# One of four token tiles leaves the dense products of a routed expert layer: its experts' rows are gathered and summed on VectorE

## The chip, the cores and the metric

One core of a Trainium2 chip runs the whole program as one launch. The metric is device time in microseconds (us), the median of several executions. Engines carry the names of the profile: PE (matrix products), PEld (loading of PE's stationary operand), DVE (VectorE), ACT (ScalarE), POOL (GpSimd) and SP, whose queue issues most DMAs.

## The reference, cut to what matters

The program is a block of two layers (mixer, then a routed expert layer called PEER) over 256 tokens `x` and 256 context tokens, followed by a second block of two layers over `x` alone. The change is in the PEER of layer 0. For each token, eight heads each pick 16 of 16,384 experts, and the output is a weighted sum of the rows of the picked experts:

```
def chunk(xc):
    q = (xc @ w_q).reshape(PEER_CHUNK, PEER_HEADS, 2, PEER_HALF)
    s = jnp.einsum('thid,hikd->thik', q, sub_keys).astype(jnp.float32)
    s1, i1 = lax.top_k(s[:, :, 0], PEER_TOPK)
    s2, i2 = lax.top_k(s[:, :, 1], PEER_TOPK)
    ...
    top_s, pos = lax.top_k(cand, PEER_TOPK)
    eidx = jnp.take_along_axis(cidx, pos, axis=-1)
    gate = jax.nn.softmax(top_s, axis=-1)
    u = u_emb[eidx]
    hid = jax.nn.gelu(jnp.einsum('td,thkd->thk', xc, u))
    wgt = (gate * hid.astype(jnp.float32)).astype(xc.dtype)
    return jnp.einsum('thk,thkd->td', wgt, v_emb[eidx])
```

So a token needs 128 rows of `u_emb` and 128 rows of `v_emb`, each of 1024 float32 (4 KB).

## The kernel before, in words

**Products in float32.** Every weight tile is 128x1024 float32 (512 KB). SP's queue brings it (`raw`), ACT copies it to a rounded high part `wh` (L209), and DVE, or for some tiles POOL, subtracts to get the low part `wl` (L220). `W.pool_every` says which tiles' `wl` goes to POOL. A product is then three matmuls (`mm3`, L443 to L445: high by high, low by high, high by low).

**PEER of layer 0** works on four token tiles of 128 columns: tiles 0 and 1 are `x`, tiles 2 and 3 the context; T = 512. It doesn't gather. It computes all 16,384 experts for all tokens, and the picked ones are singled out by a matrix that is zero elsewhere:

- *Queries* (`wq`, 16 weight tiles). Beside them `topk_keys` takes the top 16 of each of 16 key groups and each token tile on DVE (L1282 to L1287).
- *The u stage*, 128 weight tiles of 24 matmuls over 512 columns each. ACT applies gelu (L1460), and the result goes to DRAM (`gel_d`). Beside it runs `route()`: candidate sums `cand` on POOL (L1309), top 16 on DVE (L1316 to L1320), index look-up by one-hot compare, multiply and reduce on DVE (`eq`, L1334 to L1337). Then the gate matrix is built, four tokens a flush: DVE makes `Am`, `Bk`, `Bm` (L1395 to L1402), PE does eight 128x128 float16 matmuls (L1379), ACT evicts to `gst` (L1380), and a DMA takes it to DRAM (`g_d`); 128 flushes in all. Still in this stage, 56 tiles of the modulation weights (`modt`: 8 of layer 0, 48 of layer 1) are each multiplied by two vectors and summed, two DVE instructions each (`mod_tile`, L491, `sjunk`).
- *The vv stage*, 128 weight tiles of 24 matmuls of 512 columns (L1497; 6 for each of four token tiles). The hidden values and gates come back from DRAM four tiles at a time (`gelc` L1421, `gmc` L1423), POOL multiplies them (`wmul`, L1430), ACT and DVE split the product (`Wh` L448, `Wl` L449).

After that, `mixer(1)` begins with 24 conv and 16 gate projections of 256 columns (`tproj`, 24 matmuls each), with elementwise work on DVE beside them (L718 to L727). Between its conv projections the context rows are normalised (`norm_ctx`, called after its first and second conv step).

**What sets the order.** Weight tiles stand in one planned list (`plan`). Side work is written as generators that a small planner (`Side`) advances after each group of matmuls (`tick`): before, by a fixed period, so many steps spread over the u stage. Each engine's queue is in the order in which the program emits instructions.

Of the kernel before, what the change touches and what calls it, by code (L numbers as in the profile page):

```python
# [10 lines left out]
F32 = mybir.dt.float32  # L11
# [8 lines left out]
D = 1024  # L20
# [17 lines left out]
AY = 10  # L38
# [18 lines left out]
LATE = [i for i in range(16, 118) if i % 2 or i % 20 == 0]  # L57


def mod_late(i):  # L60
    n = LATE.index(i)
    return (0, 40 + n) if n < 8 else (1, n - 8)
# [11 lines left out]
def plan():  # L74
# [9 lines left out]
    for l in range(NL):  # L84
# [29 lines left out]
        for i in range(128):  # L114
            order.append(("u", l, i))
            if l == 0 and i in LATE:
                order.append(("modt",) + mod_late(i))
        for i in range(128):
            order.append(("vv", l, i))
    for l in range(NL):  # L120
# [139 lines left out]
RATE = {"a": (50.0, 0.92), "v": (80.0, 1.04), "p": (100.0, 2.2)}  # L260


class Side:
# [8 lines left out]
    def __init__(self, period, ring):  # L272
        self.lanes, self.lates = [], []
        self.period, self.ring = period, ring
        self.now = self.due = 0.0
        self.slot = [0.0] * 4
        self.free = {"a": 0.0, "v": 0.0, "p": 0.0}
        self.seq = 0
        self.floor = False

# [19 lines left out]
    def use(self, eng, n):  # L300

        if eng == "e":
            return self.now + SEM
        a, b = RATE[eng]
        self.free[eng] = max(self.free[eng], self.now) + a + b * n
        return self.free[eng] + SEM

# [42 lines left out]
    def tick(self, dt):  # L350
        self.now += dt
# [29 lines left out]
def tile_dit_peer_conformer(ctx: ExitStack, tc: tile.TileContext, A, out):  # L381
# [77 lines left out]
    modc = [consts.tile([128, 48, 2], F32, name=f"modc{l}") for l in range(NL)]  # L459

# [25 lines left out]
    def mod_tile(l, n, S, junk):  # L486

        raw = W.next("modt", l, n)
        for s in range(2):
            o = modc[l][:, n, s:s + 1]  # L490
            nc.vector.scalar_tensor_tensor(junk, raw, 1.0, S[:, s], op0=OP.mult, op1=OP.mult, accum_out=o)  # L491
        made.add((l, n))
# [125 lines left out]

    def tick(dt):
# [35 lines left out]
    def mixer(l, kp, norm_ctx=None, convs=None):  # L655
# [5 lines left out]
        with ExitStack() as st:  # L661
# [46 lines left out]
            for ct in range(8):  # L708
                def proj(b):
                    p = convs[b] if convs and ct == 0 else tproj(("conv", l, ct * 3 + b), X, T)  # L710
                    md(mod_slots(ct, b))
                    return p
# [16 lines left out]
                if l == 1 and ct < 2:  # L729
                    norm_ctx[ct]()  # L730
# [14 lines left out]
            for k, n in enumerate(GATES):  # L745
                g = sig(m1, ("gate", l, 16 + n))
                md(gate_slots(k, 0))
                pco = tproj(("co", l, n), CG, T)
                md(gate_slots(k, 1))
                nc.vector.scalar_tensor_tensor(merged[:, n], g, 1.0, pco[:, :T], op0=OP.add, op1=OP.mult)  # L750
            phase.close()
            m2 = phase.enter_context(tc.tile_pool(name=f"mixb{l}", bufs=1))
# [384 lines left out]
            phase.close()  # L1137
            keys = kp.enter_context(tc.tile_pool(name=f"keys{l}", bufs=1, side="right")).tile([128, 16, 128], F32, name="keys")
# [63 lines left out]
    def seg_tail(pool, ns, upd, halves, hs, ss, ab, banks, fill=None, then=None):  # L1202
# [9 lines left out]
        if fill is None:  # L1212
# [3 lines left out]
            rest(*range(2, 2 * ns))  # L1216
# [14 lines left out]
    def peer(l, hcp, kp, keys, early):  # L1231
        last = l == NL - 1
        T = 256 if last else 512
        nt = T // 128
        ns = T // 256
        TB = 32
        ntb = T // TB
        CI = 2048 // T
        gel_d = [dram.tile([128, CI, T], F32, name=f"gel{l}_{c}") for c in range(128 // CI)]
# [3 lines left out]
        with ExitStack() as st:  # L1243
            pp = st.enter_context(tc.tile_pool(name=f"peer{l}", bufs=1))
            IT = pp.tile([128, 2, T], F16, name="IT")
            GT = pp.tile([128, 2, T], F16, name="GT")
            GN = pp.tile([128, nt, 128], F32, name="GN")
            IN = pp.tile([128, nt, 2, 128], F32, name="IN")
# [5 lines left out]
            if l == 0:  # L1254
                ms_stack = ExitStack()
                ms = ms_stack.enter_context(tc.tile_pool(name="modrow", bufs=1))
# [5 lines left out]
            tk = tk_stack.enter_context(tc.tile_pool(name=f"topk{l}", bufs=1))  # L1262
            sv = tk.tile([128, nt, 16, 16], F32, name="sv")
# [3 lines left out]

            def topk_keys():
                for c in range(16):
                    while c not in qs or (c < 2 and c + 1 not in qs):  # L1270
                        yield
                    q = qs.pop(c)
# [4 lines left out]
                    nc.scalar.activation(s, b[:, :T], AF.Copy)  # L1277
                    for t in range(nt):
                        yield
# [8 lines left out]
                    yield  # L1288
# [6 lines left out]
            side = cur["side"] = W.side = Side(24 * T / 2.4 / (nt + 1.3), ring)  # L1295
            side.add(select())
            W.pool_every = 1
            for c in range(16):
                p = early.pop(0)[0] if early else tproj(("wq", l, c), X, T)
                q = tk.tile([128, T], F32, name="q", bufs=4)  # L1300
                nc.scalar.activation(q, p[:, :T], AF.Copy)
                qs[c] = q

            def route():
                for t in range(nt):
                    v4 = sv[:, t].rearrange("p (h i) k -> p h i k", i=2)
                    cand = tk.tile([128, 8, 16, 16], F32, name="cand", bufs=1)
                    for h in range(8):
                        nc.gpsimd.tensor_add(cand[:, h], v4[:, h, 0, :, None].to_broadcast([128, 16, 16]),  # L1309
                                             v4[:, h, 1, None, :].to_broadcast([128, 16, 16]))  # L1310
                    ts = tk.tile([128, 8, 16], F32, name="ts", bufs=2)
                    pos = tk.tile([128, 8, 16], U32, name="pos", bufs=2)
                    yield
                    for h in range(8):
# [6 lines left out]
                        yield TKW  # L1321
                    ab = tk.tile([128, 2, 8, 16], U32, name="ab", bufs=2)
                    nc.vector.tensor_scalar(ab[:, 0], pos, 4, None, op0=OP.logical_shift_right)
                    nc.vector.tensor_scalar(ab[:, 1], pos, 15, None, op0=OP.bitwise_and)
                    abf = tk.tile([128, 2, 8, 16], F32, name="abf", bufs=2)
                    nc.vector.tensor_copy(abf, ab)
                    sif = tk.tile([128, 8, 2, 16], F32, name="sif", bufs=2)
                    nc.vector.tensor_copy(sif, si[:, t].rearrange("p (h i) k -> p h i k", i=2))
                    yield
                    for i in range(2):  # L1330
                        for h0 in (0, 4):
# [6 lines left out]
                            yield TKW * 1.3  # L1338
                    nc.vector.tensor_sub(GN[:, t].rearrange("p (h k) -> p h k", h=8), ts, ts[:, :, 0:1].to_broadcast([128, 8, 16]))
                nc.scalar.activation(GN, GN, AF.Exp)  # L1340
                sm = tk.tile([128, nt, 8], F32, name="smx")
                for t in range(nt):
                    g = GN[:, t].rearrange("p (h k) -> p h k", h=8)
                    nc.vector.tensor_reduce(sm[:, t], g, axis=AX.X, op=OP.add)
                nc.vector.reciprocal(sm, sm)
                for t in range(nt):
                    g = GN[:, t].rearrange("p (h k) -> p h k", h=8)
                    nc.vector.tensor_mul(g, g, sm[:, t, :, None].to_broadcast([128, 8, 16]))
                yield
                yield  # L1350
                yield
                for i in range(3):
                    b = bankB()
                    for t in range(nt):
                        src = GN[:, t] if i == 2 else IN[:, t, i]
                        nc.tensor.transpose(b[:, t * 128:(t + 1) * 128], src, ident)
                    if i < 2:
                        nc.scalar.activation(IT[:, i], b[:, :T], AF.Copy)
                        continue
                    gw = tk.tile([128, T], F32, name="s", bufs=2)  # L1360
                    nc.scalar.activation(gw, b[:, :T], AF.Copy, scale=GSCALE)
                    nc.scalar.activation(GT[:, 0], gw, AF.Copy)
                    nc.vector.tensor_sub(GT[:, 1], gw, GT[:, 0])
                W.pool_every = 0
# [6 lines left out]
                def flush(q, Am, Bm):  # L1371
# [8 lines left out]
                    nc.scalar.activation(sg[:, :, r * 4:r * 4 + 4].rearrange("p i t -> p t i"),  # L1380
                                         b.rearrange("p (t i) -> p t i", t=4), AF.Copy, scale=1.0 / GSCALE)
                    if r == TB // 4 - 1:
                        nc.scalar.dma_start(g_d[tb], sg)

# [831 lines left out]
```

## Time and profile before

| | |
|---|---|
| median of three runs | 4619.03 us (4615.78, 4619.03, 4619.39) |
| profiled execution | 4620.17 us, of which the span of the trace is 4618.4 us |
| PE busy | 4520.1 us (98%) |
| DVE busy | 3002.5 us (65%) |
| ACT busy | 2022.4 us (44%) |
| POOL busy | 959.8 us (21%) |
| DMA | 831.69 MB, 180 GB/s mean |

The profile gives each engine's busy time, the span in 40 slices, the DMA queues, the chain that ended last and groups of instructions by line. The trace behind it also answers for any stretch: busy time by stretch, who waited for whom, and single instructions in order of time. Times in stretches count from the span's start.

### The profile page before, as it was taken

Reading aid. Unit: us, or ns where it says so; the run is one execution under the profiler, and the core shown is the slowest. Engines: PE = TensorE matmul, PEld = TensorE weight load, DVE = VectorE, ACT = ScalarE, POOL = GpSimd, SP = SyncE. Lnnn points to the kernel's source line nnn. Section 1 sums busy time; section 2 is a strip of 40 time slices with the busy share of each in tenths; the row PEclk is TensorE's granted clock in tenths of the full one; section 3 lists DMA queues with packets and bytes.
Section 4 is the critical chain, followed back from the end, with each engine's and each line's share of the span. In section 5 each row is a group of like instructions: output and inputs, shape, how many; then the busy total and the mean of one; then the engine's idle time right before and its main releaser. Section 6 shows DMA issues by size and latency. Waiting matters only on the chain. (4 is left out here: it accounts for less than half of the span.)

```text
span 4618.4 us, 67755 instructions
## 1 busy us (share of the span) xinstructions
PE 4520.1 (98%) x26426; PEld 3890.3 (84%) x26426; DVE 3002.5 (65%) x4853; ACT 2022.4 (44%) x2955; POOL 959.8 (21%) x772
## 2 busy tenths in 40 slices
PE   8999999999999999999999989999999999999999
PEld 5887878887777888888898879999887998999988
DVE  6747768899987333333365878786666577555855
ACT  4224443224665322222244444576444445444544
POOL 0012433331001322222222446201443000000000
PEclk9999999999999999999999989999999999999999
DMA  5532232455667655555543336678886644556344
GB/s 213 167 99 67 71 107 87 142 187 203 252 248 254 203 193 192 186 184 187 165 152 122 101 121 205 225 272 304 286 282 234 211 152 128 187 178 210 116 157 154
DMA packets 284922, 831.69 MB, mean 180 GB/s; under 512 B 23720, under 2 KB 108088, under 8 KB 275128
## 3 DMA queue, kind: packets, MB, share of 16 engines
q1 hardware_dynamic: 260384, 713.64, 47.0%
q10 hardware_dynamic: 24040, 112.66, 6.5%
q8 instruction: 207, 3.39, 0.3%
q14 instruction: 115, 0.94, 0.1%
q0 software_dynamic: 176, 1.06, 0.1%
HBM read 724.50 MB, written 102.77 MB: 179 GB/s over the span
## 5 line engine op out<-in xcount | busy, mean ns | idle before, releaser
L220 DVE TENSOR_TENSOR wl<-raw,wh 128x1024 fp32r<-128x1024 f32 (+1 forms) x959 | 1206.3, 1267 | 844.3 <-PE pB L1497 340.7
L209 ACT ACTIVATE wh<-raw 128x1024 fp32r<-128x1024 f32 (+1 forms) x1086 | 1131.8, 1045 | 1075.8 <-issue 697.8
L443 PE MATMUL pA<-xH,wh 128*128 128x256 f32 (+1 forms) x4600 | 1504.0, 327 | 2.9 <-ACT xH L448 1.3
L445 PE MATMUL pA<-xH,wl 128*128 128x256 f32 (+1 forms) x4600 | 1480.2, 322 | 4.7 <-DVE wl L220 3.0
L444 PE MATMUL pA<-xL,wh 128*128 128x256 f32 (+1 forms) x4600 | 1479.0, 322 | 0.5 <-DVE xL L449 0.3
L445 PEld LDWEIGHTS pA<-xH,wl 128*128 128x128 f32 x4600 | 872.7, 190 | 77.8 <-DVE wl L220 4.6
L443 PEld LDWEIGHTS pA<-xH,wh 128*128 128x128 f32 x4600 | 870.4, 189 | 75.7 <-issue 6.0
L444 PEld LDWEIGHTS pA<-xL,wh 128*128 128x128 f32 x4600 | 870.4, 189 | 68.8 <-DVE xL L449 1.1
L1430 POOL TENSOR_TENSOR gelc<-gelc,gmc 128x512 f32<-128x512 f32 (+1 forms) x256 | 333.8, 1336 | 982.1 <-DMA gmc<-gmat 663.6
L220 POOL TENSOR_TENSOR wl<-raw,wh 128x1024 fp32r<-128x1024 f32 (+1 forms) x127 | 316.0, 2488 | 874.9 <-PE pA L445 499.0
L1497 PE MATMUL pA<-wh,Wh 128*128 128x512 f32 x1024 | 322.5, 395 | 0.0
L1497 PE MATMUL pA<-wl,Wh 128*128 128x512 f32 x1024 | 322.5, 395 | 0.0
L1497 PE MATMUL pA<-wh,Wl 128*128 128x512 f32 x1024 | 322.5, 395 | 0.0
L444 PE MATMUL pA<-wl,xH 128*128 128x256 f32 (+2 forms) x800 | 271.6, 339 | 8.6 <-POOL wl L220 6.0
L443 PE MATMUL pA<-wh,xH 128*128 128x256 f32 (+2 forms) x800 | 277.4, 347 | 1.1 <-ACT xH L448 1.0
L1380 ACT ACTIVATE gst<-pB 128x512 f32<-128x512 f32 x192 | 215.1, 1126 | 140.3 <-PE pB L1379 139.6
L449 DVE TENSOR_TENSOR Wl<-gelc,Wh 128x512 fp32r<-128x512 f32 (+1 forms) x256 | 162.4, 635 | 169.7 <-ACT Wh L448 167.7
L445 PE MATMUL pA<-wh,xL 128*128 128x256 f32 (+2 forms) x800 | 270.9, 339 | 1.1 <-DVE xL L449 1.1
L1460 ACT ACTIVATE gstage<-pA 128x512 f32<-128x512 f32 x192 | 117.1, 610 | 289.0 <-PE pA L445 276.4
L1497 PEld LDWEIGHTS pA<-wh,Wl 128*128 128x128 f32 x1024 | 192.0, 187 | 47.0
L1497 PEld LDWEIGHTS pA<-wl,Wh 128*128 128x128 f32 x1024 | 192.0, 188 | 46.8
L1497 PEld LDWEIGHTS pA<-wh,Wh 128*128 128x128 f32 x1024 | 192.0, 188 | 46.7
(425 smaller groups left out, 6004.2 us busy)
## 6 DMA issues: line engine op xcount, KB each, us to landing
raw<-in_u SPq DMA_DIRECT2D x256, 512.0 KB, 4.2
raw<-in_vv SPq DMA_DIRECT2D x256, 512.0 KB, 3.7
gel<-gstage ACTq DMA_DIRECT2D x96, 512.0 KB, 4.0
gmat<-gst ACTq DMA_DIRECT2D x24, 2048.0 KB, 8.2
gelc<-gel SPq DMA_DIRECT2D x48, 1024.0 KB, 5.9
gmc<-gmat SPq DMA_DIRECT2D x48, 1024.0 KB, 9.6
raw<-in_modt SPq DMA_DIRECT2D x80, 512.0 KB, 4.0
raw<-in_conv SPq DMA_DIRECT2D x48, 512.0 KB, 3.6
```

What stands on the lines that cost most here:

```text
L209: self.nc.scalar.activation(h[:, :w], t[:, :w], AF.Copy)
L220: e.tensor_sub(lo[:, :w], t[:, :w], h[:, :w].bitcast(F32))
L443: nc.tensor.matmul(o, s[0], m[0], start=start, stop=False)
L444: nc.tensor.matmul(o, s[0], m[1], start=False, stop=False)
L445: nc.tensor.matmul(o, s[1], m[0], start=False, stop=stop)
L449: nc.vector.tensor_sub(lo, src, h.bitcast(F32))
L1380: nc.scalar.activation(sg[:, :, r * 4:r * 4 + 4].rearrange("p i t -> p t i"), b.rearrange("p (t i) -> p t i", t=4), AF.Copy, scale=1.0 / G ...
L1430: nc.gpsimd.tensor_mul(gv, gv, m[:, :, ci])
L1460: nc.scalar.activation(gs[:, j:j + n].rearrange("p a t -> p (a t)"), b, AF.Gelu_apprx_tanh)
L1497: nc.tensor.matmul(acc[t][dh], s_, m_[:, dh * 512:(dh + 1) * 512], start=(i == 0 and n == 0), stop=(i == 127 and n == 2))
```

## The change: what it does

Token tile 3, the second context tile, leaves the dense products of layer 0's PEER. TD = 384 columns stay in the u stage, three token tiles (18 matmuls for a weight tile) in the vv stage, 96 flushes in the gate matrix; `gel_d` and `g_d` shrink by a quarter. `route()` handles tile 3 first and turns its picks into expert numbers `gi`. A generator `gathered()` then takes, for each of the 128 picks, one row of `u` for each of the 128 tokens by an indirect DMA issued on POOL (512 KB, into one of four buffers `gr`), and a DVE instruction forms the dot products with the tokens' rows `gx`; then gelu and gate; then the same with rows of `v`, which a DVE instruction adds, times the weight, to the accumulator. That is 256 indirect DMAs and 256 DVE instructions over 128x1024. `gx`, the tile's rows, comes from 16 small matmuls.

With it: the planner knows DVE's and ACT's rates and fills DVE up to its estimated end (`spend`, `RATE2`, `pe = 1.09`); `cand` goes from POOL to DVE; `wmul` goes from POOL to one DVE instruction of 128x1536 for four tiles; layer 1's 48 modulation tiles go from the u stage to the vv stage, 32 of them with one column in place of two; the tables of `angles` (POOL) go from the u stage's end to its last tiles and the vv stage; the `wl` of the vv stage stays on DVE. What is left of the gathers at the end of the vv stage is spread over the first 34 projections of `mixer(1)` (`tail`, `TAIL = 35`); tile 3's update comes at projection 34, the context's row factors at 35, its columns at 38.

```diff
-LATE = [i for i in range(16, 118) if i % 2 or i % 20 == 0]
...
+LATE = [60 + 7 * i for i in range(8)]
+def late_v(i):
+    n = (i - 1) * 48 // 122
+    return (n,) if 0 < i <= 122 and n < i * 48 // 122 else ()
...
+RATE2 = {"a": (120.0, 0.92), "v": (165.0, 1.04), "p": (100.0, 2.2)}
+NG = 4
+GLAT = 4500.0
+TAIL = 35
...
-        for s in range(2):
+        for s in range(2 if l == 0 or n < 16 else 1):
...
+                if tail:
+                    tail(ct * 3 + b, m1)
...
-                if l == 1 and ct < 2:
-                    norm_ctx[ct]()
...
+        TD = T - 128 if sp else T
+        ntd = TD // 128
...
+            def gathered():
+                tabs = (A["ur"], A["vr"])
...
+                        nc.gpsimd.indirect_dma_start(t, None, tabs[j // 128], bass.IndirectOffsetOnAxis(ap=gi[:, k:k + 1], axis=0))
+                        rows[j] = (t, side.free["v"] + GLAT)
...
+                for j in range(128):
+                    yield step(1.0, rows[j][1])
+                    r = rows.pop(j)[0]
+                    nc.vector.scalar_tensor_tensor(r, r, 1.0, gx, op0=OP.mult, op1=OP.mult, accum_out=gz[:, j:j + 1])
...
+                    fetch(j + NG)
+                nc.scalar.activation(gz, gz, AF.Gelu_apprx_tanh)
...
+                for j in range(128):
+                    yield step(1.0, rows[128 + j][1])
...
+                        nc.vector.scalar_tensor_tensor(acc, r, gz[:, j:j + 1], acc, op0=OP.mult, op1=OP.add)
...
+                    fetch(128 + j + NG)
...
-                for t in range(nt):
+                for t in (range(nt) if not sp else (3, 0, 1, 2)):
...
+                    nc.vector.tensor_mul(gv, gv, m.rearrange("p b c t -> p c b t"))
...
-                    mm3(o, (h[:, d * 128:(d + 1) * 128], lo[:, d * 128:(d + 1) * 128]), (X[0][:, d, :T], X[1][:, d, :T]), d == 0, d == 7)
-                    tick(3 * T / 2.4)
...
+                    mm3(o, (h[:, d * 128:(d + 1) * 128], lo[:, d * 128:(d + 1) * 128]), (X[0][:, d, :TD], X[1][:, d, :TD]), d == 0, d == 7)
+                    tick(3 * TD / 2.4)
...
-                for t in range(nt):
+                for t in range(ntd):
                     vmm(t, i, w, hl)
...
+            while ga["n"] < 256 and (256 - ga["n"]) * TAIL > (TAIL - 1 - n) * todo:
+                next(gat_gen, None)
```

On DVE, in the middle of layer 0's vv stage, two instructions a weight tile stood before (`wl` is the low part of the weight tile, `Wl` that of the hidden values):

```order
L449 TENSOR_TENSOR Wl<-gelc,Wh 128x512
L220 TENSOR_TENSOR wl<-raw,wh 128x1024
```

and at the same place there are now gathers (`gr`), modulation (`sjunk`) and the gate product (`gmc`) between them:

```order
L1604 TENSOR_TENSOR gelc<-gelc,gmc 128x1536
L473 TENSOR_TENSOR Wl<-gelc,Wh 128x384
L223 TENSOR_TENSOR wl<-raw,wh 128x1024
L1408 SCALAR_TENSOR_TENSOR gr,gz<-gr,gx 128x1024
L516 SCALAR_TENSOR_TENSOR sjunk,modc_98<-raw,S 128x1024 x2
L473 TENSOR_TENSOR Wl<-gelc,Wh 128x384
L223 TENSOR_TENSOR wl<-raw,wh 128x1024
L473 TENSOR_TENSOR Wl<-gelc,Wh 128x384
L223 TENSOR_TENSOR wl<-raw,wh 128x1024
L1408 SCALAR_TENSOR_TENSOR gr,gz<-gr,gx 128x1024 x2
```

A `wl` that PE will load now stands behind up to four instructions over 128x1024 where it stood behind one over 128x512.

On DVE, in the conv projections at the head of `mixer(1)`, before:

```order
L220 TENSOR_TENSOR wl<-raw,wh 128x1024
L718 TENSOR_TENSOR upad_18242<-pA,tmpa 128x256
L722 TENSOR_SCALAR tmpb<-upad_18242,pcol 128x256
L724 SCALAR_TENSOR_TENSOR tmpb<-upad_18242,pcol,tmpb 128x256 x2
L727 SCALAR_TENSOR_TENSOR tmpb<-tmpb,pA 128x256
L449 TENSOR_TENSOR cgL<-tmpb,cgH 128x256
L220 TENSOR_TENSOR wl<-raw,wh 128x1024 x2
```

and now, with the last gathers of the second half (`gx` is the accumulator):

```order
L223 TENSOR_TENSOR wl<-raw,wh 128x1024
L1423 SCALAR_TENSOR_TENSOR gx<-gr,gz,gx 128x1024 x2
L223 TENSOR_TENSOR wl<-raw,wh 128x1024
L1423 SCALAR_TENSOR_TENSOR gx<-gr,gz,gx 128x1024
L750 TENSOR_TENSOR upad_17554<-pA,tmpa 128x256
L223 TENSOR_TENSOR wl<-raw,wh 128x1024
L1423 SCALAR_TENSOR_TENSOR gx<-gr,gz,gx 128x1024 x2
L754 TENSOR_SCALAR tmpb<-upad_17554,pcol 128x256
L756 SCALAR_TENSOR_TENSOR tmpb<-upad_17554,pcol,tmpb 128x256 x2
L759 SCALAR_TENSOR_TENSOR tmpb<-tmpb,pA 128x256
L473 TENSOR_TENSOR cgL<-tmpb,cgH 128x256
```

One or two gather instructions have come between each pair of `wl`.

## Rows read from the trace of the kernel before

**Rows 1.** The page's head: span; busy us of each engine, share, instructions.
```profile
span 4618.4 us, 67755 instructions
PE 4520.1 (98%) x26426; PEld 3890.3 (84%) x26426; DVE 3002.5 (65%) x4853; ACT 2022.4 (44%) x2955; POOL 959.8 (21%) x772
```

**Rows 2.** Busy time by stretch: queries, u stage, vv stage, first projections of mixer(1).
```profile
core 0: us, PE busy (x) PEld busy (x) DVE busy (x) ACT busy (x) POOL busy (x), PEclk, DMA share, GB/s
717.00:816.00 99.00, 99.00 (x503) 82.89 (x502) 85.49 (x437) 33.15 (x47) 36.03 (x15) 1.00 0.27 86
816.00:1600.90 784.90, 784.90 (x4114) 621.23 (x4113) 631.05 (x1001) 353.52 (x402) 152.08 (x157) 1.00 0.62 213
1600.90:2320.30 719.40, 718.92 (x3089) 577.49 (x3087) 285.18 (x270) 206.60 (x267) 178.28 (x122) 1.00 0.55 183
2326.00:2449.00 123.00, 118.17 (x953) 116.72 (x953) 78.83 (x112) 57.30 (x83) 21.35 (x19) 0.97 0.56 175
```

**Rows 3.** Waits, 700 to 2480 us, PE; then 1605 to 2300 us, DVE.
```profile
engine line waited for: us in total, times, longest us
PE pA L444 <- DVE xL L449: 2.4, 5, 0.7
PE pA L445 <- DVE wl L220: 1.9, 2, 1.1
...
DVE wl L220 <- PE pB L1497: 333.5, 123, 2.8
```

**Rows 4.** Timeline, PE: first and 48th of consecutive 384-column matmuls, second block.
```profile
start us, us, engine line op out<-in xcount [idle before <-releaser]
3799.71 0.34 PE L443 MATMUL pA<-wh,xH 128*128 128x384 f32 x1
...
3807.85 0.34 PE L445 MATMUL pA<-wh,xL 128*128 128x384 f32 x1
```

**Rows 5.** Busy time in a stretch, PE, the gate-matrix matmuls (L1379) alone.
```profile
1108.00:1480.00 372.00, 81.03 (x1024) 1.00 0.69 249
```

**Rows 6.** Groups by line and shape, u and vv stage (816 to 2320 us).
```profile
line engine op names shapes xcount | busy us, mean ns | idle before us <-releasers
L220 DVE TENSOR_TENSOR wl<-raw,wh 128x1024 fp32r<-128x1024 f32 x229 | 309.8, 1353 | 470.2 <-PE pB L1497 340.7 <-PE pA L445 61.5 <-issue 35.4
L491 DVE SCALAR_TENSOR_TENSOR sjunk<-raw,S 128x1024 f32<-128x1024 f32 x112 | 152.1, 1358 | 1.9
L220 POOL TENSOR_TENSOR wl<-raw,wh 128x1024 fp32r<-128x1024 f32 x25 | 63.5, 2541 | 189.9 <-PE pA L445 147.9 <-DVE IN L1337 14.5 <-ACT wh L209 9.3
L1334 DVE TENSOR_TENSOR eq<-abf,iota 128x1024 f32<-128x1024 f32 x16 | 25.8, 1612 | 0.2
L1336 DVE TENSOR_TENSOR eq<-eq,sif 128x1024 f32<-128x1024 f32 x16 | 22.3, 1394 | 0.5
L1337 DVE TENSOR_REDUCE IN<-eq 128x64 f32<-128x1024 f32 x16 | 19.5, 1220 | 0.6
```

**Rows 7.** The same view, DVE, 1110 to 1470 us, where POOL does nothing.
```profile
L220 DVE TENSOR_TENSOR wl<-raw,wh 128x1024 fp32r<-128x1024 f32 x53 | 64.8, 1223 | 26.7 <-issue 16.2 <-ACT gst L1380 9.8 <-PE pA L445 0.3
L491 DVE SCALAR_TENSOR_TENSOR sjunk<-raw,S 128x1024 f32<-128x1024 f32 x59 | 72.0, 1221 | 1.0
L491 DVE DVE_READ_ACCUMULATOR sjunk<-raw,S 128x1 f32 x59 | 4.8, 81 | 0.0
```

**Rows 8.** Timeline, vv stage: DVE alone at 2267, beside POOL at 2272 us.
```profile
2267.00 1.23 DVE L220 TENSOR_TENSOR wl<-raw,wh 128x1024 fp32r<-128x1024 f32 x1 [2.78 <-PE pB L1497]
2269.13 0.69 DVE L449 TENSOR_TENSOR Wl<-gelc,Wh 128x512 fp32r<-128x512 f32 x1 [0.90 <-ACT Wh L448]
...
2272.48 5.24 POOL L1430 TENSOR_TENSOR gelc<-gelc,gmc 128x512 f32<-128x512 f32 x3 [15.71 <-DMA gmc<-gmat]
2272.60 2.26 DVE L220 TENSOR_TENSOR wl<-raw,wh 128x1024 fp32r<-128x1024 f32 x1 [2.78 <-PE pB L1497]
2274.78 1.78 DVE L449 TENSOR_TENSOR Wl<-gelc,Wh 128x512 fp32r<-128x512 f32 x1
```

**Rows 9.** DMA by stretch (us, PEclk, share, GB/s): two peaks, one vv burst.
```profile
10.00:30.00 20.00, 0.93 1.03 418
3180.00:3200.00 20.00, 1.00 1.03 400
...
1908.00:1910.00 2.00, 1.00 0.95 400
1910.00:1912.00 2.00, 1.00 1.04 303
1912.00:1914.00 2.00, 1.00 1.12 381
```

**Rows 10.** DMA issues (KB each, median us to landing), and POOL's one in the timeline.
```profile
raw<-in_vv SPq DMA_DIRECT2D x256, 512.0 KB, 3.7
merged<-in_crow POOLq DMA_DIRECT2D x1, 1024.0 KB, 5.4
...
63.92 0.81 POOL L700 DMA_DIRECT2D merged<-in_crow  x1
```

More of the change, by code (lines that the diff above doesn't have):

```diff
@@ L303, in use, with spend, finish, once @@
             return self.now + SEM
-        a, b = RATE[eng]
-        self.free[eng] = max(self.free[eng], self.now) + a + b * n
+        a, b = self.rate[eng]
+        return self.spend(eng, a + b * n)
+    def spend(self, eng, ns):
+        self.free[eng] = max(self.free[eng], self.now) + ns
         return self.free[eng] + SEM
+    def finish(self, gen):
+        while self.active(gen):
+            self.once(gen)
+    def once(self, gen):
+        lane = next(x for x in self.lanes if x[0] is gen)
+        r = self._ready(lane[1])
+        assert r < INF
+        self.now = max(self.now, r)
+        self._run(lane)
     def begin(self, gen, done):
@@ L617, in use, with spend @@
             cur["side"].use(eng, n)
+    def spend(eng, ns):
+        if cur["side"] is not None:
+            cur["side"].spend(eng, ns)
     def tick(dt):
@@ L653, in h_update, with mixer @@
         stat(pool, h, ss[:, t % 2, hf:hf + 1], hf)
-    def mixer(l, kp, norm_ctx=None, convs=None):
+    def mixer(l, kp, tail=None, convs=None, xp=None, done=None):
         last = l == NL - 1
@@ L1215, in seg_tail @@
             W.pump(3)
-            rest(*range(2, 2 * ns))
+            if ns == 2:
+                rest(2)
             return
@@ L1266, in peer, with step, took @@
             qs = {}
+            def step(cost=1.0, ready=0.0, may=None, banks=0, hold=0.0, pe=0.0):
+                return (ready, may, banks, hold, 0.0, pe) if sp else cost
+            def took(eng, ns):
+                return cur["side"].spend(eng, ns) if sp and cur["side"] else 0.0
             def topk_keys():
                 for c in range(16):
-                    while c not in qs or (c < 2 and c + 1 not in qs):
-                        yield
-                    q = qs.pop(c)
+                    if sp:
+                        yield step(1.0, lambda: qs[c][1], lambda: c in qs, 1, 1800.0, 1100.0)
+                    else:
+                        while c not in qs or (c < 2 and c + 1 not in qs):
+                            yield
+                    q = qs.pop(c)[0]
                     b = bankB()
@@ L1298, in peer, with gat_rows @@
+            def gat_rows():
+                for hf in range(2):
+                    p = bankA()
+                    for j in range(4):
+                        for k in range(2):
+                            nc.tensor.matmul(p[:, j * 128:(j + 1) * 128], X[k][:, hf * 4 + j, TD:T], idr, start=k == 0, stop=k == 1)
+                    nc.scalar.activation(gx[:, hf * 512:(hf + 1) * 512], p, AF.Copy)
+                    took("a", 650)
             for c in range(16):
                 p = early.pop(0)[0] if early else tproj(("wq", l, c), X, T)
-                q = tk.tile([128, T], F32, name="q", bufs=4)
+                while sp and len(qs) == NQ:
+                    side.once(sel)
+                q = tk.tile([128, T], F32, name="q", bufs=NQ)
@@ L1345, in route @@
[L1345 to L1351, printed above, removed]
+                            took("v", 3700)
+                            yield step(TKW * 1.3)
+                    nc.vector.tensor_sub(GN[t].rearrange("p (h k) -> p h k", h=8), ts, ts[:, :, 0:1].to_broadcast([128, 8, 16]))
@@ L1478, in peer @@
                     wmul(0)
-            acc = [[None, None] for _ in range(nt)]
-            for t in range(nt):
+            acc = [[None, None] for _ in range(ntd)]
+            for t in range(ntd):
                 for dh in range(2):
```

299 lines of the change are left out of this document (222 added, 77 removed).

## The prediction

> **What bounds the kernel now.** I read the page's head first [rows 1]: PE is busy for 98% of the span, so a change helps only by shortening PE's own work or hurts by making PE wait. Then the stretches of layer 0's expert layer [rows 2]: in the u stage (784.9 us) and the vv stage (719.4 us) PE is busy without a gap at a granted clock of 1.00, which is the 2.4 GHz level. In the same stretches DVE works for 631.05 and 285.18 us. The waits say the same from the other side [rows 3]: between 700 and 2480 us PE's longest wait sums to 2.4 us, while in the vv stage DVE waits 333.5 us for PE to free a buffer. So there is unused DVE time, most of it in the vv stage, and PE time is what the change takes out.
>
> How PE's time goes with columns: the vv stage has 3089 matmuls, nearly all of 512 columns, in 719.4 us [rows 2], so 232.9 ns each. In the second block 48 matmuls of 384 columns in a row start over 3807.85 − 3799.71 = 8.14 us [rows 4], 47 steps of 173.2 ns. PE's time follows the columns, and weight loading doesn't set the pace at 384.
>
> **What the change takes from PE.** The u stage has 128 x 24 = 3072 matmuls that go from 512 to 384 columns: 3072 x (232.9 − 173.2 ns) = 183 us. The vv stage loses 128 x 6 = 768 matmuls of 512 columns: 768 x 232.9 ns = 179 us. Of the 1024 gate-matrix matmuls, 81.03 us [rows 5] and so 79 ns each, 256 go: 20 us. The 16 small matmuls for `gx` cost 16 x 79 ns = 1 us. Together **PE gains 381 us**. It is what would be won if everything added stayed hidden.
>
> **What is added, stage by stage.** A DVE instruction over 128x1024 with two inputs takes 1.22 us when POOL is still, and 0.08 us more where it returns a sum [rows 7]. From 0.69 us at 512 columns [rows 8] and 1.22 at 1024 the others follow: 0.56 us for 384 (`Wl`), 1.76 for 1536 (`wmul`). The order of the new program says how many stand in each stage; 12, 24, 31, 132 and 56 of the 255 repeated gather instructions stand in the five below.
>
> *Routing, at the head of the u stage.* DVE has some 203 us of work beside 50 weight tiles of 24 x 173.2 ns = 4.16 us, 208 us of PE. That is as good as full, and these are the instructions that POOL lengthens: `eq` takes 1.61 us and the multiply after it 1.39, where the reduction, with one input, takes 1.22; `wl` takes 1.35 over both stages [rows 6] against 1.22 with POOL still [rows 7]. 16 x 0.39 + 16 x 0.17 + 25 x 0.13 = 12 us more, and POOL still computes half of `wl` here. 215 against 208, and with the indirect DMAs as further POOL work I take a **loss of 12 us**, bounds 0 and 25 (twice that excess).
>
> *Gate matrix.* DVE 277 us beside 292 of PE (56 tiles of 4.16 and 768 matmuls of 79 ns). 15 us of cover; the planner may still put a `wl` late. **3 us**, between 0 and 15.
>
> *The rest of the u stage.* 14 tiles, 58 us of PE; 31 gathers and 13 `wl` are 31 x 1.30 + 13 x 1.22 = 56 us of DVE. But their transfers are 31 + 14 times 0.52 MB, with stores and first loads of the vv stage some 29 MB. The best stretch of 20 us moved 418 GB/s at a share of 1.03 [rows 9]; 29 MB take 69 us at that. **Loss 11 us**; at most 22, by the 361 GB/s of the burst below.
>
> *The vv stage.* PE: 128 x 18 x 232.9 ns = 537 us. DVE: 129 `wl` of 1.23, 61 first-half gathers and 64 modulation instructions of 1.30, 71 second-half gathers of 1.22, 128 `Wl`, 31 `wmul`, which with small ones are 538 us. DMA: 129 weight tiles, 132 gathers and 48 modulation tiles of 0.52 MB and 49 MB of hidden values and gates are 211 MB. The old vv stage moved 183 GB/s at a share of 0.55 [rows 2]. In a burst in which the DRAM tiles of hidden values come in, the rate at full share was (400 + 303 + 381) / 3 = 361 GB/s [rows 9]; where only weights come, 400 to 418. With 49 MB at 361 and 162 MB at 410 the transfers take 531 us; all at 361 they take 584. So three resources each have 531 to 538 us of work. None has slack to make up for the moments in which another is late, since each works through buffers a few tiles deep: `wl` now stands behind as many as four long DVE instructions, and PE waits behind `wl`. If all keep step the loss is 0; at the burst's rate it is 47. I take **30 us**, nearer the upper end, because the burst's row is the one that contains this mix.
>
> *The projections of `mixer(1)`.* Here the stage before was 123 us with 78.83 of DVE [rows 2], 3.08 us a projection. Now 56 gathers stand in the first 34: 68.5 us. DVE there has 31 `wl` (38 us), the gathers, and elementwise work that was there before (28 us): 135 us against 34 x 24 x 118 ns = 96 of PE (256 columns at half the pitch of 512). DVE is the bound, and the rest of the stage adds 6 x 3.08: 154 us where 123 were. **Loss 31 us**; 24 if the new work only adds to the old sum (78.83 + 68.5 = 147), 41 if four `wl` on POOL of 2.54 us each [rows 6] come on top. The context's normalisation, moved behind it, has the gate projections as cover.
>
> The step to the weights' queue: layer 1's modulation tiles only move from one stage of SP's list to the next, and count above. POOL loses 188 us of `wmul` and holds the gathers' issues in order with `angles`; each issue waits for DVE to free one of four buffers, and nothing that PE needs stands behind it until the projections.
>
> **Sum.** 4620.2 − 381 + 12 + 3 + 11 + 30 + 31 = 4326 us against the profiled execution, 1 us less against the median: I say **4325**.
>
> **Rivals.** *All covers hold* and only the projections pay: 4619 − 381 + 31 = 4269. For it: no DVE wait now delays PE by more than a microsecond. Against: three stages are planned to the brim.
>
> *Transfers bound the vv stage throughout.* For it: 0.55 of share moved only 183 GB/s [rows 2], so full share might move 183 / 0.55 = 333, and rows scattered over a table may cost more than weight tiles in a row. 211 MB then take 634 us, a loss of 97 in place of 30, and 29 MB take 87, 29 in place of 11: 4410. Against: the share also counts packets that wait, and the peaks reach 400 and more. The Trainium skill ("SBUF — State Buffer", section "Summary: rules for kernel authors") says to reckon with about 358 GB/s between DRAM and SBUF; by that the vv stage would take 211 / 0.358 = 589 us, a time near 4350 by estimate. The trace has higher rates for weights alone, and nearly that figure in the burst.
>
> *Issuing on POOL slows DVE.* With POOL at work a `wl` takes 2.26 us for 1.23, and a `Wl` 1.78 for 0.69 [rows 8]. POOL's one DMA issue in this trace shows 0.81 us [rows 10]. If each of 255 indirect issues holds up the DVE instruction beside it by 0.5 us, 132 x 0.5 = 66 us come in the vv stage, 28 in the projections, 16 in the rest of the u stage, which its transfers hide in part, and 6 in the routing, in all some 105 us: 4430. Against: an issue may touch other storage than an elementwise instruction. The Trainium skill (same page, "Who interferes with whom") has a DVE instruction with two SBUF inputs contend with POOL instructions that read SBUF, and the second to come blocks wholly; the rows on `wl` agree, and none shows an indirect issue. By it a wait is bounded by the issue's reading part.
>
> *Gathers come too slowly, and it ends slower than before.* If an indirect DMA is served every g us, the stages with 132, 31 and 56 gathers take at least 132 g, 31 g and 56 g, against 537, 58 and 96 us of PE. The loss 219 g − 691 reaches the gain when g = 4.9 us. From there on the kernel is slower. With four buffers that would need 4 x 4.9 = 19.6 us from issue to data. If gathers went one after another, each at the 5.4 us of POOL's one DMA [rows 10], the loss is 492: 4730. Against: that DMA moved twice the bytes, ordinary loads of 512 KB land in 3.7 us [rows 10], and four may be under way. For it: this trace has no indirect DMA, and each makes 128 scattered requests that POOL must write out.
>
> **How the numbers follow.** The forecast (4295 to 4350) 0.42; all covers hold 0.13; transfers bound 0.18; POOL slows DVE 0.19; gathers too slow 0.06; the change doesn't do what it says, with PE's stages no shorter because the loads of `wl` set their pace, 0.02. A measurement of this kernel tells some 0.2%, 9 us, from no change. The first four are all faster, 0.92; slower 0.06; same 0.02. The range goes from 4265 (all covers hold) to 4450 (POOL's case with the upper bound of the routing); what lies outside is slower, same and the far ends of the last two faster cases.
>
> **What would show it.** In the changed kernel's trace: 384-column matmuls in the u stage about 173 ns apart, 18 for a tile in vv; the u stage with gate matrix near 785 − 203 + 26 = 608 us; a vv stage of 565 us with PE's waits on `wl` (DVE) and on weight tiles spread through it; 154 us for the 40 projections, PE waiting for DVE there. An indirect DMA that lands in under 12 us says that the gathers keep up; a gather instruction of 1.3 us says that POOL doesn't hold DVE up, one of 1.8 that it does. A DMA share over 0.95 through the vv stage would speak for the transfers. The forecast is wrong if PE waits in vv sum to under 10 or over 60 us, or if the projections take less than 140 or more than 170.

## The result, and the profile after

The changed kernel takes **4540.47 us** (median of four runs, 4526.68 to 4543.78) against 4617.4 for the kernel before (four runs): a ratio of 0.9828, with a 95% interval of 0.9807 to 0.985. It is 1.7% faster, the way that was forecast, but by 77 us where 294 were forecast, and the time lies 90 us above the top of the range.

The page's head of the changed kernel, which answers to [rows 1], and its queue of indirect DMAs:

```profile
span 4538.0 us, 66430 instructions
PE 4215.3 (93%) x25423; PEld 3735.4 (82%) x25423; DVE 3221.3 (71%) x5177; ACT 1970.2 (43%) x2939; POOL 1128.6 (25%) x871
...
q0 software_dynamic: 37040, 135.29, 8.3%
```

PE's busy time fell by 305 us, the span by 80. So PE now stands idle, and even its busy time fell by less than the 381 us of the sum. The busy time by stretch shows where. First the changed kernel: u stage, vv stage, 40 projections of `mixer(1)`, rest; then the kernel before, the same four, with the edges read from the first and last matmuls of each stage (columns as in [rows 2]).

```profile
807.90:1444.10 636.20, 605.72 (x3905) 585.14 (x3903) 569.91 (x994) 313.13 (x380) 196.73 (x136) 0.98 0.71 253
1444.10:2212.60 768.50, 611.85 (x2320) 479.30 (x2320) 507.04 (x635) 197.00 (x274) 233.77 (x193) 0.87 0.80 276
2212.60:2392.00 179.40, 139.15 (x1000) 132.63 (x1000) 156.31 (x175) 61.89 (x91) 91.00 (x69) 0.90 0.77 271
2392.00:4538.00 2146.00, 2087.74 (x14353) 1917.94 (x14352) 1448.24 (x2305) 1089.10 (x1655) 417.54 (x331) 0.98 0.59 194
```

```profile
812.40:1600.90 788.50, 788.50 (x4132) 624.24 (x4131) 634.37 (x1018) 355.05 (x405) 154.28 (x158) 1.00 0.61 213
1600.90:2320.40 719.50, 719.02 (x3089) 577.49 (x3087) 285.28 (x271) 206.60 (x267) 178.28 (x122) 1.00 0.55 183
2320.40:2449.20 128.80, 122.79 (x983) 120.65 (x983) 83.02 (x118) 61.45 (x89) 22.91 (x19) 0.97 0.54 168
2449.20:4618.40 2169.20, 2114.86 (x14362) 1943.88 (x14360) 1446.85 (x2305) 1089.54 (x1655) 415.12 (x331) 0.98 0.58 192
```

The u stage won 152 us. The vv stage, from which 768 of 3072 matmuls were taken, became 49 us *longer*. The projections became 51 us longer, and code that the change doesn't touch became 23 us shorter. With 4.5 us at the queries that is the 80 us.

In the vv stage of the changed kernel no engine looks full: DVE works 507 of 768 us and the DMA share is 0.80. The waits show what the busy share hides (who waited for whom, us in total, times, longest), for all engines in that stage:

```profile
ACT wh L212 <- DMA raw<-in_vv: 515.3, 102, 10.8
POOL gr L1399 <- DVE gx L1423: 252.2, 48, 16.0
DVE gelc L1604 <- DMA gmc<-gmat: 243.9, 29, 10.4
...
PE pA L1692 <- DVE wl L223: 150.4, 31, 7.8
```

The third row is the one that decides. DVE stands still for 243.9 us, 29 times, in front of `wmul` (L1604), until the gates have come from DRAM; 507 + 244 = 751 of the stage's 768 us. One of these waits in the timeline of DVE:

```profile
1719.79 1.21 DVE L1408 SCALAR_TENSOR_TENSOR gr<-gr,gx 128x1024 f32<-128x1024 f32 x1
1720.93 0.08 DVE L1408 DVE_READ_ACCUMULATOR gr<-gr,gx 128x1 f32 x1
1730.02 1.76 DVE L1604 TENSOR_TENSOR gelc<-gelc,gmc 128x1536 f32<-128x1536 f32 x1 [9.00 <-DMA gmc<-gmat]
1731.69 0.55 DVE L473 TENSOR_TENSOR Wl<-gelc,Wh 128x384 fp32r<-128x384 f32 x1
1732.16 1.22 DVE L223 TENSOR_TENSOR wl<-raw,wh 128x1024 fp32r<-128x1024 f32 x1
```

and the same moment on PE:

```profile
1727.78 0.63 PE L1692 MATMUL pB<-wh,Wl 128*128 128x512 f32 x2
1728.24 0.63 PE L1692 MATMUL pA<-wh,Wh 128*128 128x512 f32 x2
1733.43 1.22 PE L1692 MATMUL pA<-wl,Wh 128*128 128x512 f32 x2 [4.56 <-DVE wl L223]
1734.45 1.05 PE L1692 MATMUL pA<-wh,Wl 128*128 128x512 f32 x2
1735.31 1.05 PE L1692 MATMUL pA<-wh,Wh 128*128 128x512 f32 x2
```

SP issued that gate DMA at 1716.9 us; `wmul`, one weight tile later in the program, began at 1730.0. DVE is in order, so the `wl` behind it came at 1732, and PE, having used up the tiles in hand, waited 4.56 us. After the wait a pair of matmuls takes 0.86 us (1734.45 to 1735.31) where it took 0.46 before (1727.78 to 1728.24). The granted clock of that moment is 0.50, the 1.2 GHz level, where it was 1.00 ahead of the wait (columns as in [rows 2]):

```profile
1722.00:1728.80 6.80, 6.80 (x30) 5.20 (x28) 0.00 (x0) 1.42 (x2) 0.22 (x1) 1.00 1.06 371
1733.40:1737.00 3.60, 3.56 (x8) 2.81 (x9) 3.60 (x5) 0.63 (x3) 0.72 (x1) 0.50 0.49 146
```

The 0.87 in the stage's row is the mean of many such moments.

### The profile page after: what moved, and what is told of

It is laid out like the page before. It is cut to its first block, busy times and chain, and to the rows that moved or that the text cites. A ratio compares the mean times of both kernels' runs of the same rounds, so it can differ in the third digit from the quotient of the medians.

```text
span 4538.0 us, 66430 instructions
## 1 busy us (share of the span) xinstructions
PE 4215.3 (93%) x25423; PEld 3735.4 (82%) x25423; DVE 3221.3 (71%) x5177; ACT 1970.2 (43%) x2939; POOL 1128.6 (25%) x871
## 5 line engine op out<-in xcount | busy, mean ns | idle before, releaser
L469 PE MATMUL pA<-xH,wl 128*128 128x256 f32 (+2 forms) x4600 | 1422.0, 309 | 57.3 <-DVE wl L223 46.1
L223 DVE TENSOR_TENSOR wl<-raw,wh 128x1024 fp32r<-128x1024 f32 (+2 forms) x956 | 1185.5, 1249 | 365.2 <-issue 185.5
L467 PE MATMUL pA<-xH,wh 128*128 128x256 f32 (+2 forms) x4600 | 1439.6, 313 | 1.7 <-ACT xH L472 1.3
L468 PE MATMUL pA<-xL,wh 128*128 128x256 f32 (+2 forms) x4600 | 1417.2, 308 | 0.5 <-DVE xL L473 0.3
L1692 PE MATMUL pA<-wl,Wh 128*128 128x512 f32 x1024 | 349.9, 424 | 150.4 <-DVE wl L223 150.4
L1692 PE MATMUL pA<-wh,Wl 128*128 128x512 f32 x1024 | 344.5, 419 | 1.7 <-DVE Wl L473 1.7
L1399 POOL DMA_INDIRECT gr<-in_ur,gi x128 | 185.8, 1451 | 530.9 <-DVE gr L1408 498.8
L1399 POOL DMA_INDIRECT gr<-in_vr,gi x128 | 176.3, 1377 | 340.1 <-DVE gx L1423 297.7
L1609 POOL TENSOR_TENSOR gelc<-gelc,gmc 128x256 f32<-128x256 f32 x128 | 147.9, 1189 | 422.4 <-DMA gmc<-gmat 398.6
L1692 PEld LDWEIGHTS pA<-wh,Wl 128*128 128x128 f32 x1024 | 206.8, 202 | 54.5 <-DVE Wl L473 2.4
```

What stands on the lines that cost most here:

```text
L223: e.tensor_sub(lo[:, :w], t[:, :w], h[:, :w].bitcast(F32))
L467: nc.tensor.matmul(o, s[0], m[0], start=start, stop=False)
L468: nc.tensor.matmul(o, s[0], m[1], start=False, stop=False)
L469: nc.tensor.matmul(o, s[1], m[0], start=False, stop=stop)
L1399: nc.gpsimd.indirect_dma_start(t, None, tabs[j // 128], bass.IndirectOffsetOnAxis(ap=gi[:, k:k + 1], axis=0))
L1609: nc.gpsimd.tensor_mul(gv, gv, m[:, :, ci])
```

## The experiments

Four explanations stood against each other. **A**: DVE waits in order at `wmul`, and what PE needs stands behind it. **B**: the transfers as such bound the vv stage. **C**: they do so once A is gone. **D**: DVE's own work bounds it once A is gone. The table gives the program's time and each stage's length, cut as above. The times of before, changed and e8 are medians of four runs; the others are single runs.

| kernel | time, us | u | vv | projections |
|---|---|---|---|---|
| before | 4617.4 | 788.5 | 719.5 | 128.8 |
| changed | 4540.5 | 636.2 | 768.5 | 179.4 |
| product two tiles later (e1) | 4349.6 | 633.3 | 593.2 | 176.6 |
| and loads two tiles earlier (e2) | 4408.8 | 634.6 | 643.1 | 179.8 |
| product back on POOL (e3) | 4460.1 | 640.3 | 746.4 | 126.0 |
| changed, without gather DMAs (e4) | 4364.5 | 609.2 | 635.3 | 167.9 |
| e1 without gather DMAs (e5) | 4271.0 | 609.2 | 545.9 | 166.2 |
| e1 without gathers (e6) | 4224.9 | 604.6 | 544.2 | 123.5 |
| e1, product and loads one tile earlier (e8) | 4345.7 | 637.7 | 579.1 | 179.8 |

**The product two weight tiles later (e1).**

```diff
-                if r == 0 and c + 1 < nch:
+                if r == (2 if sp else 0) and c + 1 < nch:
                     wmul(c + 1)
```

> Edit: in layer 0's vv stage the gate product (wmul, one DVE instruction for the next four tiles) is emitted two weight tiles later, just ahead of the split that reads it; nothing else moves. Theory A (DVE waits in order for the gate tile's DMA at the gate product, about 8.4 us in each of 29 chunks, and the wl that PE needs stands behind it): the DMA now has three tiles, some 12.6 us, before DVE asks for it, against the 13 to 14 us that it takes from issue to the product; the waits fall from 244 us to under 60, the vv stage from 769 to about 590 us, the program to about 4365 us. Theory B (the transfers themselves bound the vv stage, 209 MB at 278 GB/s): the time stays within 15 us of 4540, and the waits move to the weight tiles.

Measured: 4349.6 us, vv 593.2. One moved line gave back 191 us (178 by the four later runs below). DVE's wait at `wmul` went from 243.9 us in the stage to 1.7 in the whole program:

```profile
L1604 DVE TENSOR_TENSOR gelc<-gelc,gmc x32: 1747/1752/1796, 1435.9 to 1998.6; 128x1536 f32<-128x1536 f32 x32
...
  DMA gmc<-gmat: 1.7, 1
```

(the instructions of one line: count, shortest/median/longest ns; below, the wait ahead of it). A holds, B falls. Four more runs of the same kernel give 4362.59 us (4356.34 to 4367.91), a ratio of 0.9449 (0.9433 to 0.9465) to the kernel before, as expected:

> The kernel with the late gate product again, timed against the kernel before: 4335 to 4365 us, a ratio of 0.939 to 0.946.

**One part alone, in the kernel before (e7).** In the old kernel `wmul` becomes one DVE instruction at its old place:

```diff
                 g, m = ld[c]
+                if l == 0:
+                    gv = g.rearrange("p c (b t) -> p c b t", t=TB)
+                    nc.vector.tensor_mul(gv, gv, m.rearrange("p b c t -> p c b t"))
+                    return
```

> Edit: the kernel before, with one part of the change alone: in layer 0 the gate product of four weight tiles is one DVE instruction (128x2048) in place of four on POOL, emitted at the same place. Theory A: DVE now waits where POOL waited; the gate tile lands 9.6 us after its issue and one weight tile of 5.6 us lies between issue and product, so DVE waits 3 to 6 us in each of 30 chunks, 90 to 180 us in sum. PE has split tiles in hand for part of that: the program loses 0 to 80 us, 4617 to 4700. If the order on DVE is harmless, DVE's wait for the gate tile is under 30 us in sum and the time is within 5 us of the kernel before.

Its vv stage, and a wait of DVE in it:

```profile
1600.90:2320.40 719.50, 719.02 (x3089) 577.12 (x3087) 311.82 (x302) 206.59 (x267) 1.13 (x2) 1.00 0.55 183
...
DVE gelc L1430 <- DMA gmc<-gmat: 152.6, 30, 5.7
```

DVE waits 152.6 us, within what A expects, and the stage is not a tenth of a microsecond longer (the program took 4623.8 us, 9 above the kernel before in a run beside it, none of it here). DVE had 719 us for 312 of work, and catches up 5 us at a time while PE works from the tiles in hand. So the wait costs nothing by itself. That it costs where DVE has no slack is seen next, in e4 against e5.

**Gathers without their transfers (e4, e5).** The same cut in the changed kernel and in e1: only the first four of 256 indirect DMAs are issued.

```diff
                 def fetch(j):
+                    if j >= NG:
+                        rows[j] = (ga["t"][j % NG], side.free["v"] + GLAT)
+                        return
```

> Edit: the changed kernel, but only the first four indirect DMAs are issued; the 252 others are left out and the DVE instructions run on the first four buffers again (so tile 3's output is not the function's, and a factor 0.125 keeps the numbers finite). All DVE, ACT and PE instructions stay, the gate product stays at its early place. Theory A (DVE waits in order for the gate tile's DMA): the wait stays but gets shorter with less traffic, from 8.4 to some 4 to 6 us a chunk, since the same DMA landed 9.6 us after its issue in the kernel before; the vv stage goes from 769 to 640 to 690 us and the program to 4400 to 4450. Theory B (the transfers alone bound the stage): the vv stage falls to PE's 540 us and the program below 4300.

> Edit: the kernel with the late gate product, with the same indirect DMAs left out (252 of 256; tile 3's output is not the function's). Theory C (once DVE doesn't wait for the gate tile, the transfers bound the vv stage: 1.01 of DMA share at 374 GB/s in its middle, 582 us): without 69 MB the vv stage falls to 545 to 555 us, the stretch ahead of it by some 12 us, the program to 4285 to 4315. Theory D (DVE, with 538 us of its own in that stage, is what bounds it): the vv stage stays at 575 us or more and the program at 4335 to 4350.

Measured: 4364.5 and 4271.0 us. In e4 DVE's wait for the gates halves:

```profile
DVE gelc L1608 <- DMA gmc<-gmat: 125.3, 30, 7.8
```

The vv stage is 635 us, slightly under what A expected, and the program 36 us under; both are far over B. So the traffic of the gathers had lengthened the wait, but did not make it. And e4 and e5 differ by `wmul`'s place alone: with some 505 us of work on DVE in either, 125 us of waiting there cost the vv stage 89 us (635.3 against 545.9).

In e5 the vv stage is 545.9 us where e1 needs 593.2; these are the vv stages of e1 and of e5:

```profile
1438.30:2031.50 593.20, 564.20 (x2321) 445.38 (x2322) 509.00 (x636) 196.25 (x274) 239.00 (x194) 0.96 0.97 358
...
1414.20:1960.10 545.90, 541.69 (x2323) 434.87 (x2322) 507.16 (x630) 195.47 (x272) 64.40 (x66) 1.00 0.76 259
```

DVE does the same 507 to 509 us of work in both. What differs is the DMA share, 0.97 against 0.76, and PE is nearly without a gap in the second. POOL's issues are gone too (239 us of POOL's work against 64), but they had not lengthened DVE's instructions: a gather instruction takes 1231 and 1280 ns (first and second half) in e1, 1235 and 1280 in e5. C holds and D falls: in e1 transfers bound the vv stage, at 358 GB/s, near the 361 of the burst in [rows 9]. They act on a DVE that is nearly full itself: its 509 us of work and its waits, 51 for ACT's `Wh` and 27 for rows, fill 587 of the 593. The program came out 14 us below what C gave, since the stretch ahead won 24 us and not 12, and the projections 10.

**No gathers at all (e6).** In e1 the generator ends before its first DMA, so DVE's 256 instructions go too, and tile 3's expert sum is zero.

> Edit: the kernel with the late gate product, with the whole gather left out, DMAs and DVE instructions (tile 3's expert sum is zero in its place). What is left is the shorter dense work and the moved steps. If PE's gain is the 381 us of the sum, and the moved steps (modulation tiles, candidate sums, the gate product on DVE) are covered, the program takes 4215 to 4250 us, and gathers cost about 110 to 130 us in the kernel with the late product. If the moved steps themselves cost, it stays over 4270.

Measured: 4224.9 us, as expected. vv is 544.2 us, hardly under e5. So without their transfers 132 gather instructions on DVE cost that stage under 2 us. In the projections they cost 43 us (166.2 against 123.5) and their transfers 10 more.

**Loads earlier as well (e2), and both earlier (e8).** In e2 the loads of hidden values and gates move too, from the chunk's last tile to its second (`r == 1`); in e8 the product stands at `r == 1` and the loads at `r == 2`, so that as in e1 three tiles lie between.

> Edit: as the first, and the DMAs of the hidden values and gates are issued two tiles earlier (as soon as the last split of the chunk before last has been emitted), so that five tiles, some 21 us, lie between issue and product. Theory A: the waits of DVE for the gate tile vanish (under 20 us in sum), the vv stage comes to 555 to 575 us, the program to about 4335 us, the forecast. Theory B: as the first, near 4540 us.

> Edit: against the kernel with the late gate product, the product and the DMAs that it needs are both emitted one weight tile earlier; three tiles stay between issue and product, and the product is done one tile before ACT asks for it. Theory C (transfers bound the vv stage): ACT's wait for the product, 62 us in sum, goes, but the transfers stay, so the program gains at most 10 us: 4335 to 4350. If ACT's wait was what held PE, the vv stage falls from 593 to under 570 us and the program under 4330. If SP's queue, which now asks for the buffer one tile earlier, waits for DVE as it did when the load stood two tiles earlier (75 us in sum there, 4409 us), the time lies between 4350 and 4409.

e2 was a miss: 4408.8 us, 59 above e1, though DVE doesn't wait for the gates at all. The wait had moved to SP's queue. Here is the row of e2 from the waits of SP:

```profile
SPq L1595 <- DVE Wl L473: 74.7, 27, 8.2
```

The load overwrites a buffer whose last reader, `Wl`, had only just been emitted. SP stood there 27 times with the weight tiles behind it; e1 has no such row. At e8's place it is gone too, ACT's wait for the product falls from 62.1 us in e1 to 9.2, and e8 takes **4345.65 us** (4342.67 to 4347.95), a ratio of 0.9407 (0.9392 to 0.9423): the fastest complete kernel here. Its vv stage is 579 us at a share of 0.99, so transfers still fill it. It is 17 us ahead of the four later runs of e1's kernel and 4 ahead of the first; vv fell by 14, where C allowed 10 for ACT's wait. What that wait was worth stays open by some microseconds.

**The product back on POOL (e3).** `wmul` is four POOL instructions again.

> Edit: the gate product goes back to POOL, four instructions a chunk at the old place, as in the kernel before. POOL then waits for the gate tile in place of DVE. Theory A: PE's wait on wl disappears, but the gathers' issues stand behind POOL's wait and DVE instructions beside the product are lengthened (wl 2.26 for 1.23 us in the kernel before); the vv stage falls to 600 to 680 us, the program to 4380 to 4450. Theory B: near 4540 us. A third theory, that any POOL work beside a full DVE costs more than the wait did, would give over 4540.

4460.1 us, a little over what A gave, but vv, 746 us, is far over its 600 to 680. The gain is mostly in the projections: the planner, without `wmul` on DVE, puts 46 more gathers into the vv stage, and 10 are left. In vv the wait now sits on POOL, and POOL's work lengthens DVE's:

```profile
POOL gelc L1604 <- DMA gmc<-gmat: 139.1, 23, 10.7
...
L223 DVE TENSOR_TENSOR wl<-raw,wh 128x1024 fp32r<-128x1024 f32 x126 | 170.8, 1356 | 0.0
L1423 DVE SCALAR_TENSOR_TENSOR gx<-gr,gz,gx 128x1024 f32<-128x1024 f32 x115 | 159.1, 1384 | 85.0 <-DMA gr<-in_vr,gi 83.9
```

So POOL waits for the gates, POOL's products lengthen DVE's instructions, and DVE waits 84 us for rows. The third theory falls, since 4460 is under 4540; how much each of these costs was not separated.

**The 23 us in untouched code (e9).** In the kernel before, only the two small tiles of the angle tables leave the pool that lives through the whole program:

```diff
-        posi = consts.tile([128, 2], I32, name="posi")
+        posi = ap_.tile([128, 2], I32, name="posi", bufs=1)
...
-        freq = bcast_row("freq", A["freq"], 40)
+        freq = bcast_row("freq", A["freq"], 40, ap_)
```

> Edit: the kernel before, with one side effect of the change alone: the two small tiles for the angle tables (positions and frequencies) lie in the stage's own pool and not among the tiles that live through the whole program, so what is allocated after them moves to other addresses by some 330 bytes a partition. In all kernels with the change the code after layer 1's first projections, which is the same instruction by instruction, took 2139 to 2147 us in place of 2169.6. If the addresses are the cause, that stretch takes 2150 us or less here and the program 4590 to 4600; if not, it stays within 5 us of 2169.6 and the program within 8 us of the kernel before.

Measured: 4590.4 us in a single run, 28 less than the kernel before. The stretch after the projections takes 2143.3 us where it took 2169.2:

```profile
2445.40:4588.70 2143.30, 2084.95 (x14362) 1914.27 (x14360) 1453.54 (x2305) 1090.32 (x1655) 415.48 (x331) 0.99 0.57 194
```

No work and no order was changed on any engine. What changed is where tiles lie; see the last section. The granted clock can't be all of it: it is 0.98 in this stretch before and 0.99 here, but also 0.98 in the changed kernel, which takes 2146.0 us.

## Why the prediction was wrong, point by point

**What PE gains: nearly right.** 381 us were reckoned. The vv stage of e6, where little hinders PE, is 175 us shorter than before (179 reckoned). In its u stage PE's busy time fell from 788.5 to 598.0 us, by 191 (203 reckoned for matmuls and flushes). The pitches of [rows 2] and [rows 4] carried over but for some 4%.

**The step that failed: the vv stage, 30 us of loss reckoned, 231 measured** (768.5 against 537). Its sum counted `wmul` on DVE by its 1.76 us and nothing else. The wait that the instruction brought with it was left out, though the row was there: in [rows 8] POOL's `gelc` product has waited 15.71 us for `gmc<-gmat`. On POOL only further products stood behind that wait. The prediction named `wl` behind long DVE instructions, but not `wl` behind a DVE instruction that waits for a DMA. It could have been priced. The vv stage of the kernel before has this row of issues (KB each, median us from issue to landing):

```profile
gmc<-gmat SPq DMA_DIRECT2D x30, 1024.0 KB, 9.7
```

The load is issued one weight tile ahead of the product, and a tile is now 18 matmuls of 232.9 ns, 4.2 us. So by estimate some 5.5 us are left to wait in each of 31 chunks. e7 measures nearly that with the old traffic: 152.6 / 30 = 5.1 us. Thirty-one of those on a DVE with 538 us of work for 537 of PE make up to some 160 us, a total near 4450; the gathers' traffic stretched them to 8.4 (243.9 / 29).

The measured stage splits cleanly with e5's 541.69 us of PE work at a clock of 1.00. PE's busy time is 611.85 us, so 70 us are the same matmuls at a lower clock, and 157 us are idle: 542 + 70 + 157 = 769. The 150.4 us of waiting on `wl` thus came with half as much again through the clock. No term stood for that. The prediction's own signs say the same: it called itself wrong if PE's waits in vv passed 60 us or the projections 170, and they came to 157 and 179.

**The transfers: the reason right, the sizes at the upper bounds.** With the wait gone, e1 and e5 differ by 47 us in the vv stage, the upper bound of the 30, and e8 and e5 still by 33. Over PE's 537 us the loss is 56 us in e1, lower clock included, and 42 in e8. The burst's rate was the right row. The end of the u stage, from the last gate-matrix matmul on, takes 84 us in e1 and in the changed kernel and 63 in e5: 21 us, where 11 were reckoned and at most 22. The Trainium skill ("SBUF — State Buffer", section "Summary: rules for kernel authors") reckons with some 358 GB/s between DRAM and SBUF; e1's vv stage ran at 358 and e8's at 366.

**Routing and gate matrix: near.** 12 + 3 us were reckoned (by its own terms the routing overran by 215 − 208 = 7; 12 is the whole lengthening). In the changed kernel PE waits 13.5 us for `wl` before 1100 us, 11.8 of them on DVE and 1.7 on POOL, at a granted clock of 0.98, and not at all from there to 1345. The place is the one reckoned, DVE's two-input instructions beside POOL's work: from 880 to 1100 us `wl` takes 1589 ns and the `eq` multiply 1783 (means), against 1353 and 1394 in [rows 6]. The `eq` compare went the other way, 1366 for 1612.

**The projections: mechanism right, 51 us in place of 31.** DVE worked 156 us there. The sum had 135 for the first 34 projections without a gap and PE's 19 for the rest, but DVE waited 12 us for gathers' DMAs and some for ACT, and the granted clock fell to 0.90. e5 and e6 put 43 us on DVE's instructions and clock, 10 on transfers.

**The rivals.** POOL's issues do not slow DVE. This is the row of the gather instruction's group in the vv stage of the changed kernel, with 134 indirect DMAs of about 1.4 us on POOL beside it:

```profile
L1408 DVE SCALAR_TENSOR_TENSOR gr<-gr,gx 128x1024 f32<-128x1024 f32 x59 | 71.8, 1232 | 10.4 <-DMA gr<-in_ur,gi 10.4
```

1232 ns, as with POOL still [rows 7]. Gathers did not come too slowly either: DVE waited 10.4 us for them in that stage. "Transfers bound the stage throughout" was wrong as the cause of the result, but right of what comes next, at 358 GB/s and not at its 333. And the case for "all covers hold" misread [rows 3] by a little: one wait on `wl` there is 1.1 us, not under a microsecond.

So without the one wait, the kernel that was forecast exists: e1 and e8, at 4363 and 4346 us, lie in the range, 38 and 21 us above the forecast. That they come so near is in part luck: some 23 us of it are the shorter code after the projections, for which no term stood. The main error was in reading the change, not in the price of gathering.

## What to carry to other kernels

When an instruction is moved to another engine, move its wait with it in the sum: look at what it waited for in the trace of before, name what will stand behind it in the new queue, and ask whether that engine has the slack to catch up. On a DVE that was 43% busy 153 us of waiting cost nothing (e7); on one that was planned to the brim 125 us cost 89 (e4 against e5). And a load that is issued earlier to cover a wait can bring the wait back in its own queue, through the buffer that it must find free.

## What the runs showed of the hardware that was not expected

**Where tiles lie changes PE's pace.** In the second block the 256-column matmuls of the kernel before take longer than those of e9, whose instructions are the same (first the group before, then in e9):

```profile
L443 PE MATMUL pA<-xH,wh 128*128 128x256 f32 x1424 | 403.8, 284 | 0.3 <-DVE xL L590 0.3
...
L443 PE MATMUL pA<-xH,wh 128*128 128x256 f32 x1424 | 399.0, 280 | 0.3 <-DVE xL L590 0.3
```

At a granted clock of 1.00 their successive starts lie 120 ns apart before and 117 in e9 (medians). The two tiles that moved hold 8 and 160 bytes a partition. The move is worth 26 us after the projections, a part of it clock. Every kernel with the change has the same two lines and takes 2139 to 2147 us in that stretch, so most likely 23 of the 77 us that the change won are this. Which tile's address matters, and why, was not tried.

**An idle PE is a slower PE.** Right after a wait of 4.56 us a pair of 512-column matmuls took 0.86 us for 0.46. The granted clock of the whole vv stage went from 1.00 to 0.87 with 31 waits on `wl` of up to 7.8 us in 768 us.

**An indirect DMA of 128 rows of 4 KB** occupies POOL for 0.93 to 2.43 us (median 1.68 and 1.30 for the two tables) and doesn't lengthen DVE's gather instruction measurably (1232 ns, with POOL still 1221 for an instruction of the same shape).
